# A hybrid attention block: block 2's search and four query projections moved, and attention's values as the stationary operand with probabilities in two parts

## The chip, the cores and the metric

One core of one Trainium2 chip runs the whole kernel in one launch. The metric is the device time in microseconds. The engines are TensorE (PE; PEld is its weight load), VectorE (DVE), ScalarE (ACT), GpSimd (POOL) and SyncE (SP), which issues the transfers. Each works through its own queue in order.

## The reference, cut to what matters

One layer of a decoder block on 1024 positions of 1024 channels, in float32. Half of the mixer's channels go through a gate over chunks of 128 positions, the other half through attention with 8 query heads of 64 and 2 key heads. An indexer scores the keys of each query, and the 256 highest are attended. A feed-forward stage of 4096 follows.

```python
score = jnp.einsum('bth,bths->bts', wb * (IDX_HEADS ** -0.5), jax.nn.relu(dots))
score = jnp.where(causal[None], score, -jnp.inf)
_, idx = lax.top_k(score, topk)                     # topk = 256
...
logits = jnp.einsum('btkgd,btjkd->btkgj', qg, kg) * (HEAD_DIM ** -0.5)
logits = jnp.where(sel_ok[:, :, None, None, :], logits, -jnp.inf)
p = jax.nn.softmax(logits, axis=-1).astype(v.dtype)
o = jnp.einsum('btkgj,btjkd->btkgd', p, vg)
...
merged = jnp.concatenate([rms_norm(y_a, g_out_sgu), rms_norm(y_b, g_out_attn)], axis=-1)
o = jnp.einsum('bse,ed->bsd', merged, w_out)
```

## The kernel before, in words

Queries stand in eight blocks of 128; block b sees b+1 blocks of keys. The stages in order of time: modulation, first norm and key projections (to about 100 us); the indexer's scores, the gates and the searches for the 256 best keys (to about 310); attention, with the first half of the output projection in its later part (to about 545); the second half, the second norm, and from about 640 us the feed-forward stage.

No list gives the order of the instructions. A scheduler sets it for each engine from the data's dependences and from priorities (`tc.cur_priority`, a smaller number is earlier), and each engine then takes its queue in that order. Tiles live in rings of buffers: `tr` (3 PSUM buffers for transposes), `pT` (2), `yb` (3), `raw` (2).

**The searches.** Blocks 0 and 1 take all their keys. For blocks 2 to 7 `select(b)` finds the threshold bit by bit, in 15 rounds. In a round the scores at or over the trial value are counted, the count is compared, and the trial value is changed. For blocks 6, 4 and 3 (`ON_ACT`) ACT counts (L615) and DVE does the two small steps (L616, L617); for 7, 5 and 2 DVE does all three (L603, L605, L607). The table `PRI` gives each block's search its priority. A few steps after the rounds (L637 to L646) prepare the lowest bits. `search_rest` (L648) then asks whether any row needs a longer search: L650 makes `more`, a matmul (L652) makes the flag, L653 copies it to `rest`, and a branch reads it (L657, L658). The longer search behind the branch is seldom needed and is not run here. The branch stands in a critical section, at which DVE waits for the other engines. The query projections `q_proj` of the last four blocks (24 matmuls each, L301 to L304) are made to follow the flag on PE. `mask(b)` (L671 to L686) turns a threshold into the bias `BI` by five passes over the block's scores; block 7's comes behind the branch, those of 6, 5, 4, 3 and 2 among the attention of blocks 7 and 1 (`MASKS`).

**The attention.** It runs over 32 units: blocks in the order `OB` = 0, 7, 1, 6, 5, 4, 3, 2, and for each two key heads (`grp`) and two pairs of query heads. A unit's logits (L730) are two fp32r matmuls for each 512 keys, added to the bias and reduced to the extreme on DVE (L731), then exponentiated on ACT (L734). The values follow for two key blocks at a time: four transposes of probabilities on PE (L769), one copy to SBUF on ACT (L750), and for each key block and head a matmul with the transposed probabilities as weights and 64 columns of float32 values moving (L755; it is shown as two instructions). After a block's two pairs L780 divides by the sum, `finish` normalises and transposes (L709 to L713), and from unit 19 on `oproj0` projects (L807 to L809). `stack_for` prepares the queries of a later unit (L322, L391, L392).

**Splitting in two.** The kernel has matmuls on float32 operands (L755) and on fp32r operands. For the latter a float32 operand is split into an upper half, rounded to fp32r (an ACT copy), and the rest, `lo` (a subtraction on DVE or POOL: L222, L392, L713, L882).

## Time and profile before

| what | value |
|---|---|
| time, median of 3 runs | 1246.16 us (1245.63 to 1246.74) |
| time of the profiled execution | 1248.28 us |
| its span, first to last instruction | 1246.4 us |
| mean granted TensorE clock | 0.967 of full speed |
| DVE instructions shown | 1798 |
| POOL instructions shown | 304 |

The profiled execution is 2.1 us over the median of the runs, and 1.9 us of it lie outside the span. A row of a timeline gives start and length in microseconds, engine, line and operation, output and input, and in brackets how long the engine stood idle before it and what released it. The length of a matmul's row is modelled and overlaps its successor's; the distance from one start to the next tells its rate. PEclk is the clock granted to TensorE as a share of full speed.

### The profile page before, as it was taken

What the parts mean: (1) busy time and instruction counts of PE and PEld (TensorE: products, weight loads), DVE (VectorE), ACT (ScalarE), POOL (GpSimd) and SP (SyncE); (2) the same over time, 40 slices, a digit from 0 to 9 for tenths busy, and PEclk for the clock granted to TensorE, in tenths of its full rate; (3) what the DMA queues carried; (4) which work ended last, traced back from release to release, by engine and by line L of the source; (5) the groups of instructions that cost most, each with busy time, mean ns of one, the idle gap of its engine ahead of it and who ended that gap; (6) DMA issues with size and microseconds to landing.
All of it is one profiled execution on the core that took longest, in us unless ns stands there. A gap on an engine that the chain in (4) does not pass through costs nothing.

```text
span 1246.4 us, 16883 instructions
## 1 busy us (share of the span) xinstructions
PE 1164.5 (93%) x5785; PEld 985.0 (79%) x5785; DVE 873.8 (70%) x1798; ACT 671.2 (54%) x1410; POOL 209.4 (17%) x304
## 2 busy tenths in 40 slices
PE   4899989995898999899899999999999999999997
PEld 4887768884697999887687788888887888888886
DVE  7844998968478666627898775655558756876568
ACT  4554679773266755537735455555544454445452
POOL 3585605451100000012610000000000000000001
PEclk9899989996898999999999999999999999999999
DMA  9431102110000144446315753544458455533335
GB/s 343 150 93 35 52 1 64 52 64 9 1 10 29 57 161 161 172 149 215 115 60 195 269 178 127 169 143 145 161 217 331 125 188 179 197 91 99 102 98 205
DMA packets 80239, 162.41 MB, mean 130 GB/s; under 512 B 7724, under 2 KB 32920, under 8 KB 80152
## 3 DMA queue, kind: packets, MB, share of 16 engines
q1 hardware_dynamic: 80136, 161.33, 38.3%
q8 instruction: 45, 0.74, 0.3%
q14 instruction: 42, 0.34, 0.1%
q10 hardware_dynamic: 16, 0.00, 0.0%
HBM read 119.36 MB, written 41.94 MB: 129 GB/s over the span
## 4 chain that ended last, share of the span: by engine, by line
PE 51%; DVE 12%; issue 4%; DMA 3%; ACT 2%; POOL 1%; SPq 0%; DVEq 0%; POOLq 0%; ACTq 0%
PE tr L1174 8%; PE lg L1174 8%; PE mm L1174 5%; PE mm L755 4%; PE lg L991 2%; PE lg L993 2%; PE lg L992 2%; PE tr L769 2%; PE lg L730 2%; PE tr L991 2%; PE tr L993 2%; PE tr L992 2%; DVE w L882 2%; PE mm L991 1%; PE mm L993 1%
## 5 line engine op out<-in xcount | busy, mean ns | idle before, releaser
L881 ACT ACTIVATE w<-rx 128x512 fp32r<-128x512 f32 x112 | 70.7, 632 | 148.1 <-PE lg L1174 64.5
L1174 PE MATMUL tr<-w,w 128*128 128x512 f32 x504 | 134.3, 392 | 2.9 <-DVE w L882 2.9
L1174 PE MATMUL lg<-w,w 128*128 128x512 f32 x504 | 133.7, 390 | 0.0
L882 DVE TENSOR_TENSOR w<-rx,w 128x512 fp32r<-128x512 f32 x112 | 77.2, 689 | 57.8 <-ACT w L881 57.1
L301 PE MATMUL mm<-w,hT 128*128 128x512 f32 (+1 forms) x288 | 112.8, 393 | 4.7 <-ACT hT L293 3.5
L1174 PEld LDWEIGHTS tr<-w,w 128*128 128x128 f32 x504 | 95.4, 189 | 23.2 <-DVE w L882 3.4
L303 PE MATMUL mm<-w,hT 128*128 128x512 f32 (+1 forms) x288 | 111.2, 387 | 0.0
L304 PE MATMUL mm<-w,hT 128*128 128x512 f32 (+1 forms) x288 | 110.2, 384 | 1.0 <-POOL hT L294 1.0
L1174 PEld LDWEIGHTS lg<-w,w 128*128 128x128 f32 x504 | 94.9, 188 | 19.7
L1210 POOL TENSOR_TENSOR rsf<-rsf,mhalf 128x1 f32<-128x1 f32 x8 | 6.0, 752 | 605.6 <-DVE rsf L1209 605.6
L1174 PE MATMUL mm<-w,w 128*128 128x512 f32 x336 | 93.9, 389 | 0.0
L755 PEld LDWEIGHTS mm<-VV,pT 128*128 128x128 f32 x576 | 76.1, 199 | 3.8 <-ACT pT L750 1.6
L755 PE MATMUL mm<-VV,pT 128*128 128x64 f32 x576 | 76.4, 277 | 0.9 <-ACT pT L750 0.9
L1174 PEld LDWEIGHTS mm<-w,w 128*128 128x128 f32 x336 | 63.1, 188 | 13.2
L882 DVE TENSOR_TENSOR w<-b,w 128x512 fp32r<-128x512 f32 x96 | 65.7, 685 | 4.0 <-ACT w L881 4.0
L301 PEld LDWEIGHTS mm<-w,hT 128*128 128x128 f32 x288 | 55.8, 194 | 14.9 <-ACT hT L293 3.7
L730 PE MATMUL lg<-KS,qs 128*128 128x512 f32 (+5 forms) x192 | 55.3, 399 | 10.6 <-DVE mxs L731 6.0
L882 DVE TENSOR_TENSOR w<-s,w 128x512 fp32r<-128x512 f32 x56 | 38.2, 688 | 37.3 <-ACT w L881 37.3
L304 PEld LDWEIGHTS mm<-w,hT 128*128 128x128 f32 x288 | 55.0, 191 | 10.5 <-POOL hT L294 1.3
L734 ACT ACTIVATE L<-L,mxs 128x128 f32<-128x128 f32 (+7 forms) x64 | 49.2, 771 | 25.8 <-DVE mxs L731 25.6
L881 ACT ACTIVATE w<-b 128x512 fp32r<-128x512 f32 x96 | 59.4, 618 | 6.7 <-DMA b<-in_w_ff_dram 6.5
L303 PEld LDWEIGHTS mm<-w,hT 128*128 128x128 f32 x288 | 55.5, 193 | 8.5
(356 smaller groups left out, 2975.5 us busy)
## 6 DMA issues: line engine op xcount, KB each, us to landing
rx<-x_scratch SPq DMA_DIRECT2D x56, 512.0 KB, 3.5
x_scratch<-d SPq DMA_DIRECT2D x108, 256.0 KB, 3.0
ada<-in_w_ada_dram SPq DMA_DIRECT2D x48, 512.0 KB, 5.6
raw<-in_w_ff_dram SPq DMA_DIRECT2D x32, 512.0 KB, 4.1
b<-in_w_ff_dram SPq DMA_DIRECT2D x32, 512.0 KB, 4.6
x<-in_x_dram SPq DMA_DIRECT2D x16, 512.0 KB, 5.6
raw<-in_w_in_dram SPq DMA_DIRECT2D x8, 512.0 KB, 3.6
raw<-in_w_in_dram SPq DMA_DIRECT2D x16, 256.0 KB, 2.8
```

The costliest lines, as they stand in the source:

```text
L301: mm = T.matmul(p[:, :n], lh, wt[k][:, 0, :n], start=k == 0, stop=False)
L303: T.matmul(p[:, :n], lh, wt[k][:, 1, :n], start=False, stop=False)
L304: T.matmul(p[:, :n], ll, wt[k][:, 0, :n], start=False, stop=k == KD - 1)
L730: T.matmul(pl, QS[b, grp][:, q, h4 * P:(h4 + 1) * P], KS[:, grp, c0:c0 + cw], start=q == 0, stop=q == 1)
L734: ex = A.activation(L, L, AF.Exp, scale=-1.0, bias=top, accum_out=sms[:, b, h:h + 1])
L755: mm = T.matmul(po[:, o:o + 64], e[:, (si * 2 + h2) * P:(si * 2 + h2 + 1) * P], VV[:, s0 + si, grp], start=first, stop=pair == 1 and s0 + ...
L881: A.activation(hi, src, AF.Copy)
L882: eng.tensor_tensor(lo, src, hi.bitcast(F32), op=OP.subtract)
L991: ms.append(T.matmul(p, a[:, 0, k], b[:, 0, k], start=start and k == 0, stop=False, skip_group_check=more))
L992: ms.append(T.matmul(p, a[:, 0, k], b[:, 1, k], start=False, stop=False, skip_group_check=more))
L993: ms.append(T.matmul(p, a[:, 1, k], b[:, 0, k], start=False, stop=stop and k == 3, skip_group_check=more))
L1174: ms.append(T.matmul(p, x[:, qa, t * P:(t + 1) * P], y[:, qb], start=start and n == 0, stop=stop and n == 2, skip_group_check=more))
```

## The change

1. **The search.** `PRI` gives block 2 the priority 445000 (it was 460000) and lists it before block 3. In `search_rest` the four query projections are written behind the critical section, no longer ahead of it.
2. **The values.** `VV` holds each value's upper and lower half beside each other, 128 columns, in fp32r; the lower half is one more DVE subtraction in each of eight key projections. The transposed probabilities are split too: `hi` by ACT, `lo` by DVE from PSUM, or, where `on_pool` says so, by POOL from a further ACT copy in the `raw` ring. A matmul now has the 128x128 `VV` as weights and 256 columns of probabilities (two heads) moving, once for `hi` and once for `lo` (L768). What comes out has the heads' outputs transposed, upper and lower half apart. So `values_T` copies it (ACT, into the `yb` ring), transposes it in four (L787), adds the halves in a reduction (L806) and multiplies (L807). It is called one unit later, and `finish` too.
3. **Room.** Some tiles of the gates go to a pool of their own, `gp`, which is closed before the searches; the `pT` buffers, twice as large, take its place (`pe`). Temporaries in `rotary` get one buffer each, and `mxs` is halved.

```diff
-    PRI = ((7, 400000), (6, 405000), (5, 415000), (4, 445000), (3, 455000), (2, 460000))
+    PRI = ((7, 400000), (6, 405000), (5, 415000), (4, 445000), (2, 445000), (3, 455000))
...
         V.tensor_copy(rest, p[:1, :1])
-        for b in OB[4:]:
-            q_proj(b, flag)
         with tc.tile_critical():
...
+        for b in OB[4:]:
+            q_proj(b, flag)
...
-        A.activation(VV[:, j], vv, AF.Copy)
+        A.activation(VV[:, j, :, 0:64], vv, AF.Copy)
+        V.tensor_tensor(VV[:, j, :, 64:128], vv, VV[:, j, :, 0:64].bitcast(F32), op=OP.subtract)
...
-            e = p2.tile([P, 512], F32, tag="pT", name=nm("pT"), bufs=2)
-            A.activation(e[:, :wd], pt[:, :wd], AF.Copy)
+            e = pe[0].tile([P, 2, 512], F32R, tag="pT", name=nm("pT"), bufs=2)
+            hi, lo = e[:, 0, :wd], e[:, 1, :wd]
+            if on_pool(u, s0):
+                r = rp.tile([P, 2, 512], F32, tag="raw", name=nm("pr"))[:, 0, :wd]
+                A.activation(r, pt[:, :wd], AF.Copy)
+                A.activation(hi, pt[:, :wd], AF.Copy)
+                G.tensor_tensor(lo, r, hi.bitcast(F32), op=OP.subtract)
+            else:
+                A.activation(hi, pt[:, :wd], AF.Copy)
+                V.tensor_tensor(lo, pt[:, :wd], hi.bitcast(F32), op=OP.subtract)
             for si in range(cnt_s):
-                for h2 in range(2):
-                    mm = T.matmul(po[:, o:o + 64], e[:, (si * 2 + h2) * P:(si * 2 + h2 + 1) * P], VV[:, s0 + si, grp],
+                for q in range(2):
+                    mm = T.matmul(po, VV[:, s0 + si, grp], e[:, q, si * 256:si * 256 + 256], start=first,
...
+    def on_pool(u, s0):
+        b = units[u][0]
+        if b < 2:
+            return False
+        return (s0 // 2) % 2 == 0 if b > 5 else s0 == 0 if b == 5 else u % 4 < 2
...
+    def values_T(b, grp):
+        oT = p2.tile([P, 512], F32, tag="yb", name=nm("oT"), bufs=3)
+        A.activation(oT, PO[b, grp], AF.Copy)
+        p = p_tr()
+        for i in range(4):
+            T.transpose(p[:, i * P:(i + 1) * P], oT[:, i * P:(i + 1) * P], ident)
...
     def normed(dst, src, b, h, n):
         V.reciprocal(sms[:, b, h:h + n], sms[:, b, h:h + n])
-        V.tensor_tensor(dst, src, sms[:, b, h:h + n, None].to_broadcast([P, n, 64]), op=OP.mult)
+        V.tensor_reduce(dst, src, op=OP.add, axis=mybir.AxisListType.X)
+        V.tensor_tensor(dst, dst, sms[:, b, h:h + n, None].to_broadcast([P, n, 64]), op=OP.mult)
...
+        if u and u % 2 == 0:
+            values_T(*units[u - 1][:2])
         values(u)
...
-        if u % 4 == 0 and u:
+        if u % 4 == 1 and u > 1:
             finish(OB[u // 4 - 1])
```

The scheduler then puts the instructions in another order. Lines of the changed kernel are numbered a few higher: L603 becomes L608, L616 L621, L731 L737.

On DVE, block 2's search before: its rounds (`self2`) stand behind the whole of block 3's and among the first steps of block 0's attention (`qs`, `L`).

```order
L603 TENSOR_SCALAR spare_903,self2_2640<-BI_87,self2_2640 128x384
L392 TENSOR_TENSOR qs_459_3012<-tr_461_3015,qs_459_3012 128x512
L605 TENSOR_SCALAR self2_2640<-self2_2640,kds_2636 128x1
L607 SCALAR_TENSOR_TENSOR self2_2640<-self2_2640 128x1
L731 ISA L_462_3022,mxs_3010<-lg_463_3023,BI_87 128x128
L731 ISA mxs_3010 128x1
L603 TENSOR_SCALAR spare_903,self2_2640<-BI_87,self2_2640 128x384
```

On DVE, the changed kernel: rounds of block 2 (`self2`) and of block 3 (`self3`) in turn.

```order
L608 TENSOR_SCALAR spare_913,self2_2654<-BI_87,self2_2654 128x384
L610 TENSOR_SCALAR self2_2654<-self2_2654,kds_2650 128x1
L621 TENSOR_SCALAR self3_2656<-self3_2656 128x1
L612 SCALAR_TENSOR_TENSOR self2_2654<-self2_2654 128x1
L622 SCALAR_TENSOR_TENSOR self3_2656<-self3_2656 128x1
L608 TENSOR_SCALAR spare_913,self2_2654<-BI_87,self2_2654 128x384
L610 TENSOR_SCALAR self2_2654<-self2_2654,kds_2650 128x1
```

All of block 2's rounds have moved ahead of block 0's attention, and they stand between block 3's.

On DVE, the end of the searches before: the flag's input `more` and the copy to `rest` follow the last search.

```order
L650 TENSOR_SCALAR more_2637<-kds_2636 128x6
L644 MAX self2_2640<-BI_87 128x8
L653 CAST rest_2638<-tr_496_3131 1x1
L646 ISA pick_2639,self2_2640<-pick_2639,self2_2640 128x8
L646 ISA self2_2640 128x1
L656 NO_OP
L1290 UNCONDITIONAL_BRANCH
L657 TENSOR_LOAD rest_2638
L658 COMPARE_AND_BRANCH
```

On DVE, the changed kernel, the same place: the steps just ahead of the copy to `rest` belong to block 0's attention; `more` (L655) stands 31 instructions earlier, ahead of its first `qs`.

```order
L737 ISA L_487_3115,mxs_3024<-lg_488_3116,BI_87 128x128
L737 ISA mxs_3024 128x1
L764 TENSOR_TENSOR pT_494_3136<-tr_493_3133,pT_494_3136 128x256
L807 TENSOR_TENSOR yb_491_3128<-yb_491_3128,sms_3025 128x256
L805 RECIPROCAL sms_3025<-sms_3025 128x4
L822 TENSOR_SCALAR ya_495_3141<-ya_495_3141,rsa_3021 128x512
L658 CAST rest_2652<-tr_498_3156 1x1
L659 NO_OP
L1322 UNCONDITIONAL_BRANCH
L660 TENSOR_LOAD rest_2652
L661 COMPARE_AND_BRANCH
```

The copy to `rest` and the branch have moved behind block 0's attention, whose steps no longer have a search between them.

On PE, the flag and the projections before, ahead of the branch of DVE:

```order
L709 MATMUL tr_495_3123<-ident_70,ya_493_3116 128x128 x4
L652 MATMUL tr_496_3131<-ones_75,more_2637 1x1
L301 MATMUL mm_497_3134<-w_428_2448,hT_12_143 128x512
L303 MATMUL mm_497_3134<-w_428_2448,hT_12_143 128x512
L304 MATMUL mm_497_3134<-w_428_2448,hT_12_143 128x512
L301 MATMUL mm_497_3134<-w_429_2451,hT_12_143 128x512
```

And in the changed kernel:

```order
L768 MATMUL mm_492_3132<-pT_494_3136,VV_83 128x256
L714 MATMUL tr_497_3148<-ident_70,ya_495_3141 128x128
L657 MATMUL tr_498_3156<-ones_75,more_2651 1x1
L301 MATMUL mm_499_3750<-w_428_2458,hT_12_143 128x512
L303 MATMUL mm_499_3750<-w_428_2458,hT_12_143 128x512
L304 MATMUL mm_499_3750<-w_428_2458,hT_12_143 128x512
L301 MATMUL mm_499_3750<-w_429_2461,hT_12_143 128x512
```

Nothing moved here: the projections (L301 to L304) follow the flag (L652, now L657) directly, though they are written behind the critical section.

On DVE, among the masks before: block 6's mask (`self6`) beside block 7's attention.

```order
L682 SCALAR_TENSOR_TENSOR SC_877<-eq_540_3975 128x896
L731 ISA L_546_4005,mxs_3010<-lg_548_4010,BI_87,mxs_3010 128x512
L731 ISA mxs_3010 128x1
L684 TENSOR_TENSOR self6_2648<-self6_2648,SC_877 128x1
L713 TENSOR_TENSOR mT_494_3122<-tr_542_3988,mT_494_3122 128x4x128
L685 SCALAR_TENSOR_TENSOR eq_540_3975<-SC_877,self6_2648,eq_540_3975 128x896
L686 SCALAR_TENSOR_TENSOR BI_87<-BI_87,eq_540_3975 128x896
L731 ISA L_561_4072,mxs_3010<-lg_562_4073,BI_87 128x512
```

And in the changed kernel:

```order
L687 SCALAR_TENSOR_TENSOR SC_884<-eq_546_4017 128x896
L814 TENSOR_SCALAR yb_491_3128<-yb_491_3128,rsb_3023 128x512
L689 TENSOR_TENSOR self6_2662<-self6_2662,SC_884 128x1
L690 SCALAR_TENSOR_TENSOR eq_546_4017<-SC_884,self6_2662,eq_546_4017 128x896
L764 TENSOR_TENSOR pT_545_4007<-tr_544_4002,pT_545_4007 128x512
L691 SCALAR_TENSOR_TENSOR BI_87<-BI_87,eq_546_4017 128x896
L764 TENSOR_TENSOR pT_557_4064<-tr_556_4059,pT_557_4064 128x512
L737 ISA L_568_4119,sms_3025<-lg_569_4120,BI_87 128x512
L737 ISA sms_3025 128x1
```

Subtractions (L764, the lower halves of probabilities) now stand between the mask's last passes and ahead of the logits' reductions.

## Rows read from the trace of the kernel before

**Rows 1.** The page: busy time, share and instructions of each engine

```profile
PE 1164.5 (93%) x5785; PEld 985.0 (79%) x5785; DVE 873.8 (70%) x1798; ACT 671.2 (54%) x1410; POOL 209.4 (17%) x304
```

**Rows 2.** Four stretches: length; PE, PEld, DVE, ACT, POOL; clock; DMA; GB/s

```profile
346.40:398.84 52.44, 48.48 (x365) 45.25 (x363) 47.91 (x135) 34.30 (x73) 4.62 (x9) 0.93 0.02 6
398.84:426.60 27.76, 25.46 (x214) 24.70 (x213) 19.70 (x54) 21.93 (x44) 2.03 (x3) 1.00 0.31 96
426.60:524.30 97.70, 96.70 (x666) 88.71 (x665) 61.08 (x138) 53.83 (x125) 4.83 (x8) 0.98 0.42 153
524.30:545.10 20.80, 18.50 (x104) 16.61 (x105) 10.07 (x19) 10.74 (x23) 2.96 (x3) 0.84 0.37 118
```

**Rows 3.** Timeline of DVE, 268 to 322 us: start, length, ..., [idle before]

```profile
268.77 0.21 DVE L616 TENSOR_SCALAR self<-self 128x1 f32<-128x1 f32 x1 [0.95 <-ACT spare L615]
...
270.12 0.21 DVE L616 TENSOR_SCALAR self<-self 128x1 f32<-128x1 f32 x1 [0.94 <-ACT spare L615]
...
287.80 0.69 DVE L392 TENSOR_TENSOR qs<-tr,qs 128x512 fp32r<-128x512 f32 x1
288.40 0.20 DVE L605 TENSOR_SCALAR self<-self,kds 128x1 f32<-128x1 f32 x1
...
303.96 0.61 DVE L603 TENSOR_SCALAR_CACHE_REDUCE spare<-BI,self 128x384 int8<-128x384 int16 x1
...
305.06 0.61 DVE L603 TENSOR_SCALAR_CACHE_REDUCE spare<-BI,self 128x384 int8<-128x384 int16 x1
...
310.36 0.13 DVE L653 CAST rest<-tr 1x1 int32<-1x1 f32 x1
...
321.01 0.15 DVE L671 CAST seli<-self 128x1 int32<-128x1 f32 x1 [10.36 <-DVEq L656]
```

**Rows 4.** Timeline of PE, 288 to 330 us

```profile
288.54 0.90 PE L730 MATMUL lg<-KS,qs 128*128 128x128 f32 x3 [3.66 <-DVE qs L392]
...
299.63 1.00 PE L709 MATMUL tr<-ident,ya 128*128 128x128 f32 x4
310.12 0.19 PE L652 MATMUL tr<-ones,more 128*1 128x1 f32 x2 [9.48 <-DVE more L650]
...
316.47 0.39 PE L303 MATMUL mm<-w,hT 128*128 128x512 f32 x1
...
329.43 1.22 PE L730 MATMUL lg<-KS,qs 128*128 128x512 f32 x2 [5.24 <-DVE mxs L731]
```

**Rows 5.** DVE queue's waits, 310 to 322 us: ns min/median/max, first, last

```profile
L1290 DVEq EVENT_SEMAPHORE  x6: 50/50/5610, 310.9 to 317.0; - x6
```

**Rows 6.** Timeline of PE, 371 to 374 us

```profile
371.70 0.60 PE L769 MATMUL tr<-ident,L 128*128 128x128 f32 x4
372.14 1.00 PE L755 MATMUL mm<-VV,pT 128*128 128x64 f32 x8
372.95 0.96 PE L730 MATMUL lg<-KS,qs 128*128 128x256 f32 x6
373.74 1.00 PE L755 MATMUL mm<-VV,pT 128*128 128x64 f32 x8
```

**Rows 7.** DVE by line, 345 to 400 us: busy us, mean ns

```profile
L392 DVE TENSOR_TENSOR qs<-tr,qs 128x512 fp32r<-128x512 f32 x4 | 2.8, 688 | 2.5 <-ACT qs L391 2.5
...
L780 DVE TENSOR_TENSOR yb<-mm,sms 128x256 f32<-128x256 f32 x4 | 1.7, 413 | 0.0
```

**Rows 8.** Groups of POOL by line and shape, whole span

```profile
L222 POOL TENSOR_TENSOR w<-raw,w 128x512 fp32r<-128x512 f32 x32 | 43.1, 1368 | 9.0 <-ACT w L221 7.6 <-PE mm L304 1.3
```

**Rows 9.** Timeline of POOL from 205.91 us

```profile
205.91 5.04 POOL L222 TENSOR_TENSOR w<-raw,w 128x512 fp32r<-128x512 f32 x4 [2.67 <-ACT w L221]
```

**Rows 10.** Timeline of DVE, 208 to 214 us

```profile
208.48 1.25 DVE L617 SCALAR_TENSOR_TENSOR self<-self 128x1 f32<-128x1 f32 x1
209.65 2.73 DVE L454 SCALAR_TENSOR_TENSOR SC<-relu,WI,SC 128x384 f32<-128x384 f32 x2
...
213.13 0.61 DVE L454 SCALAR_TENSOR_TENSOR SC<-relu,WI,SC 128x384 f32<-128x384 f32 x1
```

## What the change will do: the prediction

> **What bounds the kernel now.** The page's first part is read first: TensorE is busy 93% of the span and VectorE 70% [rows 1]. Those are averages, so the attention, where both halves of the change lie, is cut into stretches [rows 2]. Three different limits appear. From 346.4 to 398.84 us, where the last five masks are made beside the attention of blocks 7 and 1, DVE is busy 47.91 of 52.44 us and PE 48.48 at a clock of 0.93: both are nearly full, and DVE has 4.5 us to spare. From 398.84 to 426.6 PE is busy 25.46 of 27.76 and DVE 19.70. From 426.6 to 524.3 PE is busy 96.70 of 97.70 with DVE at 61.08: only PE's work counts there. The last 20.8 us are a tail in which each engine waits for another.
>
> Ahead of them stand the searches, for which DVE's and PE's timelines are read side by side [rows 3, 4]. A round of block 3's search, whose counting runs on ACT, takes 1.35 us (268.77 to 270.12), and in it DVE waits 0.95 us. Block 2's search follows on DVE, mixed from 287.80 with the first attention block; a round alone takes 1.10 us (303.96 to 305.06). PE waits 9.48 us for the end of these searches (310.12), and after the flag DVE stands still for 10.36 us until the first mask starts at 321.01. PE next waits 5.24 us for that mask (329.43).
>
> **The search (first half of the change).** Block 2's rounds go into the gaps of block 3's: by the order of DVE, one round of each in turn. A round's DVE work for block 2 is about 1.0 us (1.10 less the time between instructions) against a gap of 0.95 us, so the pair takes 1.4 to 1.5 us a round and both searches end about 291 (block 3's alone ended at 283). Block 0's attention then runs without search steps between. Before, it took from 287.80 to about 299.6, some 11.8 us (its last transposes on PE start at 299.63 [rows 4]) with six search rounds mixed in, and much of it was waiting between engines, as PE's 3.66 us for one `qs` shows [rows 4]. Alone, with its own new steps, I take 10.5 us. The flag's copy to `rest`, which now stands behind that chain on DVE, comes at 301.5 and not at 310.36 [rows 3]: a gain of 8.9 us, of which I take **8.5**. The bounds: 12 if block 0's chain shrinks to 7 us, 4 if the chain, alone, takes 15 us.
>
> The place of the four projections is priced at nothing. The wait behind the flag holds one semaphore wait of 5.61 us that begins at 311.3 [rows 5] and so ends at 316.9. That is when the twentieth projection matmul after the flag ends (it starts at 316.47 and is shown with 0.39 us) [rows 4]: the block's end waits for projections that the scheduler put ahead of it. In the order of the changed kernel the projections still stand directly behind the flag on PE, ahead of the same branch. So the 10.36 us stay. Were that wait really to go, 5.6 us more would be won; I bound that at 0 to 5.6 and take 0, because the rows of the order are the same.
>
> **TensorE's part of the attention.** Eight old value matmuls (128x64) take 0.81 us (372.14 to 372.95) and six 128x256 fp32r matmuls 0.79 (372.95 to 373.74) [rows 6]: 0.101 and 0.132 us each. For one key block and one pair of heads four of the first give way to two of the second: 0.404 less 0.263 is 0.141, and there are 144 such pieces: 20.3 us. Added are 64 transposes at 0.11 (four in 0.44, 371.70 to 372.14 [rows 6]): 7.0. PE wins 13.3 us in all, but only what falls where PE is the limit counts.
>
> **VectorE's part.** By the order of the changed kernel 13 subtractions of 128x512 and one of 128x256 (L764) and four reductions with a product each (L806, L807) fall between the stretch's start and the end of the last mask, one more such pair moves in from before it, and four products (L780) go. A subtraction with a PSUM input takes 0.688 us [rows 7], and its successor starts 0.60 after it (287.80 to 288.40 [rows 3]). So: 13 x 0.60 + 0.34, plus five times 0.69 for the reduction (no row has one: between L780's 0.413 and L392's 0.688, and nearest the latter, for it reads 512 elements from PSUM) and 0.38 for a product, less 4 x 0.413 [rows 7]: 7.8 + 0.3 + 5.4 - 1.7 = 11.8 us. DVE then has 59.7 us of work in a stretch of 52.44. PE gains some 5 us there, so part of DVE's 4.5 idle us goes: bound below 59.7 (+7.3), above 64.2 (+11.8). I take **+10**.
>
> From 398.84 to 426.6 DVE's additions of about 5 us fit beside PE; with some 22 of the 144 pieces and 8 transposes PE wins 3.1 - 0.9: **-2**. From 426.6 to 524.3 some 64 pieces and 36 transposes are 9.0 - 4.0 = 5.0 us of PE. DVE (61.08 now) goes to some 78 us, and ACT (53.83 now) has one copy more for each chunk that POOL splits and for each `oT`. Neither becomes the limit, but the lower half now comes through DVE's or POOL's queue, the new `oT` shares the three `yb` buffers, and a transposed chunk's PSUM buffer is held for two readers. That costs 1 to 4 us of new gaps; **-3** remains. In the tail one more transpose, copy and reduction stand in the chain: **+1** (-1 to +3). In the prelude eight subtractions of 128x128 (at most 8 x 0.413 us [rows 7]) run beside key projections: **+0.5** (0 to 3.3).
>
> **What POOL takes from DVE.** POOL gets 34 subtractions; its like takes 1.368 us [rows 8]. While four such ran from 205.91 [rows 9], two DVE operations L454 with all inputs in SBUF took 2.73 us, and one of the same shape later took 0.61 [rows 10]: each was more than doubled. In the masks' stretch ten of the subtractions meet L685 and L686, whose inputs are in SBUF too. If they meet by chance, 13.7 us of POOL in some 62 us hit about a fifth of 10 us of such DVE work: +2 us, already in the 10 above as a choice past the middle of its bounds. The Trainium skill, "SBUF — State Buffer", section "Who interferes with whom", speaks against the change: a DVE instruction with two SBUF inputs and a GpSimd instruction that reads SBUF exclude each other for the whole of the first one. By that rule each of ten meetings costs up to a full subtraction, some 14 us at worst in place of 2; it fits the 2.73 us, and is a rival below.
>
> **Sum.** -8.5 + 0.5 + 10 - 2 - 3 + 1 = -2 us. The profiled execution took 1248.28 us (span 1246.4), 2.1 above the median of the runs, 1246.16. Off the median the sum gives **1244.0**. About 2.5 us (0.2%) is what a measurement here can tell from no change, so the forecast lies just inside it.
>
> **Rivals.**
> *The masks' stretch pays more (slower).* Place: DVE, 346 to 399 us. Its queue is served in order, so a lower half behind a 2 us scan holds PE's value matmuls, and POOL's subtractions hold L685 and L686. For it: DVE's 47.91 of 52.44, and the 2.73 us. Against it: PE has 5 us to catch up. Price: the upper bound of 11.8 and half a subtraction for each of ten meetings, 6.8, make some 18 in place of 10, and block 0's chain, which has the same new steps, takes 13 us, so that 6 are won in place of 8.5: -6 + 0.5 + 18 - 2 - 3 + 1 = +8.5, 1254.5. It decides once the stretch costs over 13 us. Chance 0.22.
> *The earlier flag brings little.* Block 0's chain was paced by its own waits; if it takes 15 us alone, only 4 are won: 1248.5. Chance 0.17.
> *PE's saving comes through.* The late masks are needed only when their blocks come up (block 2 is last), so DVE may fall behind them without PE waiting; then the stretch costs 3 and not 10, and the PE-bound one wins 5 and not 3: 1235. For it: PE at 96.70 of 97.70 for half of the attention. Against it: the masks stand in the same queue as the logits that PE waits for. Chance 0.21.
> *The forecast's case*, 1240 to 1248: 0.40.
>
> **Chances.** Of the forecast's case I count 0.23 as faster by over 2.5 us, 0.12 within and 0.05 slower; with the third rival 0.44 are faster; the second splits in two, within and slower; the first is slower. Together 0.44 faster, 0.22 within, 0.34 slower. The range 1234 to 1256 takes in the rivals' times and leaves out the worst of the exclusion (14 us) and the free projections' 5.6 us on top of a gain. The likeliest case's own range is 1240 to 1248.
>
> **What would show it.** Right: block 2's and block 3's search steps alternate and end near 291; `rest` is copied near 301 and the first mask starts near 312; the 5.6 us semaphore wait stays; the last mask ends about 1 us later than before, as the 8.5 gained are spent on DVE at over 95% busy; the PE-bound stretch is 2 to 4 us shorter. Wrong: the last mask over 5 us later with L685 and L686 stretched (first rival); `rest` after 305 (second); DVE under 90% busy while PE stays full (third); or no long semaphore wait behind the flag, which would mean that the projections' place did count.

## The result, and the profile after

The changed kernel takes **1289.5 us** (median of 4 runs, 1286.78 to 1293.5), the kernel before 1245.89 on the same chip: a ratio of 1.036, 95% interval 1.0323 to 1.0397. It is slower by some 44 us, where 1244.0 was forecast and 1256 was the upper end of the range. The profiled execution took 1292.05 us, its span is 1290.3.

The page of the changed kernel: busy time of the engines, and the groups that answer to L755, L730 and POOL's new one.

```profile
PE 1169.3 (91%) x5561; PEld 969.1 (75%) x5561; DVE 925.1 (72%) x1868; ACT 697.7 (54%) x1460; POOL 258.3 (20%) x338
...
L768 PE MATMUL mm<-pT,VV 128*128 128x256 f32 x288 | 62.7, 322 | 22.6 <-DVE pT L764 11.7
L735 PE MATMUL lg<-KS,qs 128*128 128x512 f32 (+5 forms) x192 | 57.7, 403 | 21.6 <-DVE sms L737 11.3
...
L761 POOL TENSOR_TENSOR pT<-pr,pT 128x512 fp32r<-128x512 f32 (+1 forms) x34 | 47.4, 1402 | 112.8 <-ACT pT L760 106.5
```

Beside [rows 1] no engine has much more to do: DVE 51 us, POOL 49, ACT 27, and all three stay under 73%. What is new is 22.6 and 21.6 us in which PE stands idle ahead of the value and logit matmuls. The page of the kernel before had 0.9 and 10.6 there:

```profile
L755 PE MATMUL mm<-VV,pT 128*128 128x64 f32 x576 | 76.4, 277 | 0.9 <-ACT pT L750 0.9
L730 PE MATMUL lg<-KS,qs 128*128 128x512 f32 (+5 forms) x192 | 55.3, 399 | 10.6 <-DVE mxs L731 6.0
```

Where PE stands idle is seen with marks on DVE's timeline: the copy to `rest`, the first mask, the last mask, block 6's second product, block 2's last.

```profile
309.04 0.15 DVE L658 CAST rest<-tr 1x1 int32<-1x1 f32 x1 [0.60 <-PE tr L657]
317.90 0.15 DVE L676 CAST seli<-self 128x1 int32<-128x1 f32 x1 [8.71 <-DVEq L659]
...
412.01 0.54 DVE L691 SCALAR_TENSOR_TENSOR BI<-BI,eq 128x384 bf16<-128x384 bf16 x1
...
448.15 0.42 DVE L807 TENSOR_TENSOR yb<-yb,sms 128x256 f32<-128x256 f32 x1
...
578.90 0.42 DVE L807 TENSOR_TENSOR yb<-yb,sms 128x256 f32<-128x256 f32 x1
```

The same marks of each run divide its span into five stages (us):

| kernel | to first mask | masks' stretch | to block 6's end | to block 2's end | rest | span |
|---|---|---|---|---|---|---|
| before | 321.0 | 77.8 | 22.6 | 117.4 | 707.6 | 1246.4 |
| **changed** | 317.9 | 94.6 | 35.6 | 130.8 | 711.4 | 1290.3 |
| e1 search only | 308.6 | 77.2 | 23.7 | 117.6 | 709.5 | 1236.6 |
| e4 lower halves all by DVE | 317.8 | 90.0 | 26.0 | 118.0 | 710.1 | 1261.9 |
| e10 as e4, idle copies | 315.9 | 92.7 | 30.0 | 125.1 | 716.2 | 1279.9 |
| e11 POOL's copies kept, DVE subtracts, own ring | 317.5 | 91.8 | 25.1 | 130.5 | 710.1 | 1275.0 |
| e8 POOL's copies kept, DVE subtracts | 316.3 | 95.2 | 31.5 | 128.2 | 713.0 | 1284.2 |
| e3 own ring, POOL subtracts | 316.1 | 96.0 | 32.0 | 131.8 | 710.8 | 1286.7 |
| e7 no lower half | 316.5 | 79.3 | 22.0 | 106.6 | 712.6 | 1237.0 |

The changed kernel wins 3.1 us before the first mask and loses 16.8, 13.0, 13.4 and 3.8 behind it. In the kernels with the changed values a block's product comes one unit later, so the mark of block 6 is not quite the same place of the work as before; the third and fourth stage taken together are safer: 140.0 us before, 166.4 changed, 144.0 in e4.

**Block 6.** Queues show best here, since everything stops for 9 us. PE's timeline of the changed kernel, 428 to 438 us:

```profile
428.15 0.60 PE L795 MATMUL tr<-ident,L 128*128 128x128 f32 x4
437.33 1.01 PE L735 MATMUL lg<-KS,qs 128*128 128x384 f32 x2 [8.57 <-DVE sms L737]
```

DVE's, of the same place:

```profile
426.94 0.69 DVE L718 TENSOR_TENSOR mT<-tr,mT 128x512 fp32r<-128x512 f32 x1 [0.15 <-ACT mT L717]
429.36 1.43 DVE L225 SCALAR_TENSOR_TENSOR wo<-raw,cols,wo 128x512 fp32r<-128x512 f32 x2 [1.73 <-ACT wo L224]
432.02 1.41 DVE L225 SCALAR_TENSOR_TENSOR wo<-raw,cols,wo 128x512 fp32r<-128x512 f32 x2 [1.23 <-ACT wo L224]
435.38 1.42 DVE L225 SCALAR_TENSOR_TENSOR wo<-raw,cols,wo 128x512 fp32r<-128x512 f32 x2 [1.95 <-ACT wo L224]
436.71 0.55 DVE L737 CUSTOM_DVE_ANT_0 L<-lg,BI 128x384 f32<-128x384 f32 x1
```

ACT's:

```profile
428.60 1.33 ACT L224 ACTIVATE wo<-raw,cols 128x512 fp32r<-128x512 f32 x2 [1.70 <-DMA raw<-in_w_out_dram]
```

And what SP's queue waited for from 380 to 460 us (us in total, times, the longest):

```profile
SPq L819 <- DVE yb L814: 67.3, 3, 28.5
SPq L207 <- POOL pT L761: 8.6, 2, 6.3
```

Read backwards: PE's logits wait for a buffer that DVE has to empty (L737), DVE's L737 stands in its queue behind the splitting of the output weights (L225), that behind ACT's (L224), that behind the weights' transfer, and SP issues that (L207) only after the load of `ya` ahead of it in its queue (L819, which waits for a `yb` buffer that DVE's late L814 holds) and after POOL has read `pr` out of the two `raw` buffers (L761). Before, two of the four transfers of these weights had been issued at 260.46 and 265.15, ahead of the attention, and the others followed at 400.80 (260.98, 266.44 and 387.72 in e1), beside work that was there anyway. With the second `raw` user and the late `yb` all four come from 424.71 on.

**What it does to PE.** Windows of the changed kernel, masks' stretch from 364 on and the three behind it (length; PE, PEld, DVE, ACT, POOL; clock; DMA):

```profile
364.25:422.54 58.29, 42.08 (x250) 33.99 (x249) 51.52 (x129) 35.58 (x78) 15.13 (x14) 0.94 0.03 10
422.54:448.15 25.61, 15.26 (x89) 13.31 (x89) 16.15 (x39) 16.73 (x33) 5.65 (x5) 0.80 0.26 83
448.15:496.98 48.83, 44.27 (x268) 37.25 (x265) 36.65 (x84) 33.84 (x75) 18.49 (x15) 0.97 0.31 108
530.17:562.93 32.76, 28.14 (x147) 22.78 (x145) 23.40 (x41) 16.88 (x41) 5.97 (x5) 0.89 0.55 185
```

The first of them runs 10 us past the last mask. Up to that mask DVE is busy 46.1 of 48.3 us, so there DVE is nearly full. Behind it no engine is, where PE was at 96.70 of 97.70 before [rows 2]; and in the second and the last window, where PE stands idle for 10.4 of 25.6 and for 4.6 of 32.8 us, the granted clock is lower as well (0.80, 0.89).

### The profile page after: what moved, and what is told of

Its sections match the earlier page's. It is cut to its first block, busy times and chain, and to the rows that moved or that the text cites. A ratio compares the mean times of both kernels' runs of the same rounds, so it can differ in the third digit from the quotient of the medians.

```text
span 1290.3 us, 16614 instructions
## 1 busy us (share of the span) xinstructions
PE 1169.3 (91%) x5561; PEld 969.1 (75%) x5561; DVE 925.1 (72%) x1868; ACT 697.7 (54%) x1460; POOL 258.3 (20%) x338
## 4 chain that ended last, share of the span: by engine, by line
PE 54%; DVE 11%; ACT 4%; DMA 3%; issue 2%; POOL 1%; SPq 0%; DVEq 0%; POOLq 0%; ACTq 0%
PE tr L1206 8%; PE lg L1206 8%; PE mm L1206 5%; PE lg L1023 3%; PE lg L1024 3%; PE lg L1025 3%; PE tr L1023 3%; PE tr L1024 3%; PE tr L1025 3%; PE mm L834 2%; PE mm L835 2%; PE mm L836 2%; PE mm L1023 2%; PE mm L1024 2%; PE mm L1025 2%
## 5 line engine op out<-in xcount | busy, mean ns | idle before, releaser
L301 PE MATMUL mm<-w,hT 128*128 128x512 f32 (+1 forms) x288 | 113.1, 394 | 9.7 <-ACT hT L293 7.3
L304 PE MATMUL mm<-w,hT 128*128 128x512 f32 (+1 forms) x288 | 110.7, 386 | 0.3 <-POOL hT L294 0.3
L768 PE MATMUL mm<-pT,VV 128*128 128x256 f32 x288 | 62.7, 322 | 22.6 <-DVE pT L764 11.7
L735 PE MATMUL lg<-KS,qs 128*128 128x512 f32 (+5 forms) x192 | 57.7, 403 | 21.6 <-DVE sms L737 11.3
L301 PEld LDWEIGHTS mm<-w,hT 128*128 128x128 f32 x288 | 55.8, 194 | 21.5 <-ACT hT L293 7.5
L768 PEld LDWEIGHTS mm<-pT,VV 128*128 128x128 f32 x288 | 45.7, 202 | 34.5 <-DVE pT L764 15.5
L761 POOL TENSOR_TENSOR pT<-pr,pT 128x512 fp32r<-128x512 f32 (+1 forms) x34 | 47.4, 1402 | 112.8 <-ACT pT L760 106.5
L304 PEld LDWEIGHTS mm<-w,hT 128*128 128x128 f32 x288 | 55.4, 193 | 9.8 <-POOL hT L294 0.6
```

The lines of the kernel that those rows point to most:

```text
L301: mm = T.matmul(p[:, :n], lh, wt[k][:, 0, :n], start=k == 0, stop=False)
L304: T.matmul(p[:, :n], ll, wt[k][:, 0, :n], start=False, stop=k == KD - 1)
L735: T.matmul(pl, QS[b, grp][:, q, h4 * P:(h4 + 1) * P], KS[:, grp, c0:c0 + cw], start=q == 0, stop=q == 1)
L768: mm = T.matmul(po, VV[:, s0 + si, grp], e[:, q, si * 256:si * 256 + 256], start=first, stop=pair == 1 and s0 + si == ns - 1 and q == 1)
```

## The experiments

**e1, the first half alone.**

```diff
-    PRI = ((7, 400000), (6, 405000), (5, 415000), (4, 445000), (3, 455000), (2, 460000))
+    PRI = ((7, 400000), (6, 405000), (5, 415000), (4, 445000), (2, 445000), (3, 455000))
...
-        for b in OB[4:]:
-            q_proj(b, flag)
         with tc.tile_critical():
...
+        for b in OB[4:]:
+            q_proj(b, flag)
```

> The kernel before with the search part alone: block 2's priority and the place of the four projections. In the changed kernel's trace the first mask starts at 317.90 us and not at 321.01. If the search part is what it looks like there, and all of the loss lies in the values, this gives 3 us less than before, 1243. If the searches beside each other cost something later, or the early flag is given back at the masks, it gives 1246 or more. If they caused part of the loss of 43 us, over 1250.

Measured: 1234.35 us beside 1243.28, ratio 0.9916 (0.9885 to 0.9947): **9 us faster by the medians, and the fastest kernel of the study that leaves nothing out.** DVE's timeline of e1:

```profile
288.78 0.16 DVE L650 TENSOR_SCALAR_CACHE_REDUCE more<-kds 128x6 f32<-128x6 f32 x1
...
299.74 0.15 DVE L653 CAST rest<-tr 1x1 int32<-1x1 f32 x1 [1.07 <-PE tr L652]
308.61 0.15 DVE L671 CAST seli<-self 128x1 int32<-128x1 f32 x1 [8.72 <-DVEq L654]
```

The searches end at 288.8, block 0's chain takes 11 us, and the flag is copied 10.6 us earlier [rows 3]. The wait at the branch stays, at 8.7 us in place of 10.36. On PE the projections follow the flag directly in either kernel, so the gain is put down to the priority; it was not run apart.

**e2, the second half alone.** `PRI` and the projections' place as before.

> The changed kernel with the search part undone: the values' part alone. If the two parts add up, 1289.5 plus the 3 us that the search part wins: about 1292. If the loss needs both (the attention of block 0 with its lower halves standing ahead of the flag), it falls clearly under 1285.

Measured: 1298.97, ratio 1.0447 (1.0401 to 1.0494). The halves roughly add up: the second half costs 55.2 us beside e1 (1289.5 less 1234.35) and 55.7 beside the kernel before (1298.97 less 1243.28). All of the loss lies in it.

**e3, a ring of its own for POOL's copies; e4, no POOL.**

```diff
-                r = rp.tile([P, 2, 512], F32, tag="raw", name=nm("pr"))[:, 0, :wd]
+                if u <= 12:
+                    r = up.tile([P, 512], F32, tag="uv", name=nm("pr"), bufs=3)[:, :wd]
+                else:
+                    r = wp.tile([P, 1024], F32, tag="w", name=nm("pr"))[:, :wd]
```

> The changed kernel, but POOL's copies of the probabilities no longer use the two raw buffers through which the weights of the output projection come: up to unit 12 they use the three buffers of the gates' and masks' scratch, later the ring of twelve. Theory of the shared ring: the loads of these weights start at 424.71 us behind the last of POOL's copies in it, ACT and DVE stand still for them and PE waits 8.57 us at 437.33; with another ring the loads start before 400 as in the kernel before, and 9 to 14 us come back: 1276 to 1281. Theory that the loss is the lower half's way through the queues: the stall is only moved, at most 4 us come back.

```diff
     def on_pool(u, s0):
         b = units[u][0]
-        if b < 2:
+        if b < 8:
             return False
```

> The changed kernel with every lower half made on DVE from PSUM: no POOL subtraction, no second ACT copy, no copy in the raw ring; 34 subtractions more on DVE (30 x 0.60 + 4 x 0.34 us, about 19 us of DVE, some 5 of it in the masks' stretch). If POOL's holding up of DVE and the shared ring are the main loss, it gives 1265 to 1275. If DVE itself is the bound of the attention, it gives 1295 or more. If both weigh alike, about the time of the changed kernel.

Measured: e3 1287.99, 1.0361 (1.0319 to 1.0402), as the changed kernel. In e3 the first two transfers of the output weights are back at 269.02 and 274.76, and PE's longest wait between 400 and 450 us is 2.8 in place of 8.57; but block 6's stage is only 3.6 us shorter, and nothing of it reaches the end. So the stall was the most visible loss and not, by itself, the cause. e4 1264.22, 1.0184 (1.0135 to 1.0233). The route that was to spare DVE work costs 25 us more than DVE doing all of it. What e4 still loses is seen in its windows (the first from 364 to 16 us past the last mask, then three pieces of the late part):

```profile
364.19:423.40 59.21, 44.85 (x257) 35.23 (x258) 58.20 (x150) 37.14 (x79) 4.46 (x6) 0.94 0.13 45
...
433.75:480.87 47.12, 45.06 (x277) 37.87 (x275) 40.06 (x99) 30.30 (x65) 4.19 (x5) 1.00 0.32 112
480.87:511.87 31.00, 29.91 (x185) 25.89 (x184) 26.08 (x55) 18.02 (x42) 3.06 (x3) 1.00 0.47 161
511.87:540.35 28.48, 24.79 (x150) 20.73 (x149) 24.16 (x47) 17.57 (x40) 1.59 (x1) 1.00 0.57 194
```

In the first DVE is full, 58.20 of 59.21. In the late part PE is busy 109.3 us (these three rows and 9.5 in the last 11.4). The late part of the kernel before:

```profile
421.39:464.19 42.80, 42.80 (x322) 40.52 (x320) 26.18 (x68) 25.26 (x56) 3.05 (x5) 1.00 0.33 112
464.19:494.58 30.39, 30.39 (x198) 27.57 (x197) 18.97 (x40) 15.83 (x38) 1.17 (x2) 0.94 0.44 165
494.58:522.20 27.62, 27.62 (x185) 24.98 (x184) 17.64 (x39) 14.84 (x38) 1.16 (x2) 1.00 0.48 182
522.20:538.78 16.58, 13.28 (x68) 11.61 (x67) 9.91 (x18) 10.81 (x22) 1.11 (x1) 0.79 0.38 120
```

PE is busy 114.1 us in it and idle 3.3; in e4 it is idle 8.8. So the saving of 4.8 stands as idle time beside it. (Part of the 4.8 is the clock's: it was granted at 0.96 before and at 1.00 in e4.)

**e8 and e11, what of the route is POOL.** POOL's subtraction is done by DVE from the same copy: in e8 with the shared `raw` ring, in e11 with e3's own ring.

```diff
-                G.tensor_tensor(lo, r, hi.bitcast(F32), op=OP.subtract)
+                V.tensor_tensor(lo, r, hi.bitcast(F32), op=OP.subtract)
```

> The changed kernel with POOL's 34 subtractions given to DVE, on the same copies: ACT still copies these probabilities twice, the first time into the raw ring, and only POOL itself is out. The kernel with all lower halves on DVE from PSUM took 1264, the changed one 1289.5. If POOL's slow subtraction and its holding up of DVE make that difference: 1264 to 1270. If the second ACT copy and the raw ring make it: 1282 to 1290. The ring's stall alone was seen as 8.57 us of PE: then about 1275.

> The kernel with POOL's 34 subtractions on DVE but the second copy left (1284.8), its copies now out of the raw ring (scratch of the masks up to unit 12, then the ring of twelve). If the raw ring holds up the output projection's weights and that is what those copies cost: 1268 to 1275. If the second copy itself is the cost: 1280 to 1285.

Measured: e8 1284.79, 1.0325 (1.0292 to 1.0358); e11 1277.5, 1.0271 (1.0232 to 1.0311), between its two theories. With e3 and the changed kernel that is a table of two by two: POOL 1289.5 and 1288.0, DVE 1284.8 and 1277.5 (shared ring, own ring). The ring alone is worth 7 us once DVE subtracts, and hardly anything beside POOL; POOL itself 5 to 10; and the second copy, which e11 still has and e4 has not, 13. (They come from several sets of runs, whose times of the kernel before lie between 1243.3 and 1245.9, so differences of 2 or 3 us are not to be read from this, and the 5 is near that limit: the intervals of the changed kernel and of e8 overlap.)

What POOL does to DVE stands in DVE's groups from 325 to 600 us. The changed kernel:

```profile
L483 DVE SCALAR_TENSOR_TENSOR adacc<-ada,cact,adacc 128x1024 f32<-128x1024 f32 x21 | 32.1, 1527 | 0.5 <-DMA ada<-in_w_ada_dram 0.2
...
L681 DVE TENSOR_TENSOR self<-seli,self 128x1 f32<-128x1 f32 x5 | 2.9, 583 | 0.0
...
L687 DVE TENSOR_TENSOR_SCAN SC<-eq 128x768 f32<-128x768 bf16 x1 | 2.8, 2819 | 0.0
...
L690 DVE SCALAR_TENSOR_TENSOR eq<-SC,self,eq 128x768 bf16<-128x768 f32 x1 | 1.9, 1921 | 0.0
```

and e8:

```profile
L483 DVE SCALAR_TENSOR_TENSOR adacc<-ada,cact,adacc 128x1024 f32<-128x1024 f32 x21 | 26.8, 1278 | 0.1
...
L687 DVE TENSOR_TENSOR_SCAN SC<-eq 128x768 f32<-128x768 bf16 x1 | 1.7, 1748 | 0.0
...
L690 DVE SCALAR_TENSOR_TENSOR eq<-SC,self,eq 128x768 bf16<-128x768 f32 x1 | 1.0, 1019 | 0.0
...
L681 DVE TENSOR_TENSOR self<-seli,self 128x1 f32<-128x1 f32 x5 | 0.8, 153 | 0.0
```

All four read two operands from SBUF. L690 takes 0.9 us longer and L687 1.1. L681, of one element a row, takes 583 ns on average in place of 153: two of its five took 1.25 and 1.24 us, the others 0.13 to 0.15. Each of these four, and one more of L690 (128x896, 2.06 us in place of 1.14), began less than 0.25 us after a subtraction of POOL's had begun. The five meetings cost DVE 5.1 us in the masks' stretch. The Trainium skill, "SBUF — State Buffer", section "Who interferes with whom", says that a DVE instruction with two SBUF inputs contends with a GpSimd instruction that reads SBUF, and calls what they share an exclusive lock; these rows agree. The dearest group is one that the prediction did not look at: L483, 5.3 us over 21 instructions. How much of either reaches the end of the kernel was not tried apart.

**e10, idle copies.** e4, with 34 further ACT copies of the same chunks that nothing reads.

```diff
+                if twice(u, s0):
+                    jk = p2.tile([P, 512], BF, tag="jb", name=nm("jk"), bufs=1)
+                    A.activation(jk[:, :wd], pt[:, :wd], AF.Copy)
                 A.activation(hi, pt[:, :wd], AF.Copy)
```

> The kernel with all lower halves on DVE from PSUM (1264), and in it 34 further ACT copies of the probabilities that nobody reads, where the changed kernel copies twice: about 20 us of ACT. If ACT's time, and the copies that wait behind in its queue, make the second copy dear: 1272 to 1285. If the copy costs only as a link of the chain (the lower half waits for both copies), nothing waits for this one: 1264 to 1267.

Measured: 1279.33, 1.0282 (1.0244 to 1.032): 15 us over e4 for copies of 19.5 us, in a kernel where ACT is busy 54%. The idle copy is written ahead of its chunk's upper half, and by the order of ACT's rows it is taken first in all 34 cases; ACT's timeline of e10 shows the first of them:

```profile
343.91 0.60 ACT L765 ACTIVATE jk<-tr 128x512 bf16<-128x512 f32 x1 [1.19 <-PE tr L804]
344.40 0.59 ACT L766 ACTIVATE pT<-tr 128x512 fp32r<-128x512 f32 x1
```

So nothing has to wait for the copy's result, and it needs neither POOL nor the `raw` ring to be dear: it is enough that it takes its turn on ACT ahead of the copy that PE's matmuls and `lo` wait for, 0.5 us where the two follow each other directly. That makes the way from probabilities to `lo` longer by one copy, as in e11. It also keeps the transposed chunk (`tr`, three PSUM buffers) longer; how the 15 us divide between the later upper half and `tr` was not tried apart.

**e7, no lower half of the probabilities.** Upper half alone: the copy, the subtraction and half of the value matmuls are left out, and with them that part of the product.

> The changed kernel without the lower half of the probabilities: no subtraction, no POOL copy, one matmul with the upper half for each key block in place of two (144 matmuls, some 19 us of PE, fewer). It leaves that part of the computation out. Values as weights, their own split, the transposes of the output and the reductions stay. Theory that the lower half's way through the queues is the loss: 1220 to 1235, under the kernel before. Theory that the new output path (copy, transposes, reduction, one unit later) costs as much: 1250 or more.

Measured: 1236.35, 0.9928 (0.9908 to 0.9949). Without the second part attention loses nothing on balance: the masks' stretch is 79.3 us, and the late part is 10.8 us shorter than before. But e7 leaves out PE's work too: PE is busy 98.8 us in the late part, 15.3 less than before, and idle 7.9 where it was idle 3.3. So it is not shown that the values as weights, the transposes of `oT` and the later `finish` cost nothing: some 4.5 us of new idle time stand there without the second part, whose cause was not tried apart. The larger loss in attention is the second part of the probabilities and what carries it.

**The prelude: e9, e12b, e13, e15.** In the changed kernel the searches end (`more`) at 296.0, in e1 at 288.8. e9 leaves out the lower half of the values (L378; the upper stands in its place); e12b gives the temporaries in `rotary` two buffers again; e13 does both; e15 does both with e4's `on_pool`.

```diff
-         A.activation(VV[:, j, :, 0:64], vv, AF.Copy)
-         V.tensor_tensor(VV[:, j, :, 64:128], vv, VV[:, j, :, 0:64].bitcast(F32), op=OP.subtract)
+         A.activation(VV[:, j].rearrange("p h (w e) -> p h w e", w=2), vv[:, :, None, :].to_broadcast([P, 2, 2, 64]), AF.Copy)
...
-            n_ = t0.tile([P, 64], F32, tag="rn", name=nm("n"), bufs=1)
+            n_ = t0.tile([P, 64], F32, name=nm("n"))
```

> The changed kernel without the eight subtractions that make the lower half of the values: ACT writes the upper half into both places, so the values' lower half is left out. In the changed trace the key projections end 5.5 us later than before, with PE idle for 4.6 us and then at half clock. If these subtractions cause that: 1283 to 1285. If it comes from the temporaries of the rotary tables with one buffer: no change, 1289.

> The changed kernel with the rotary tables' temporaries in two buffers each again (the positions' tile stays shared). In the changed trace the second half of these steps waits for the sine of the first, and the norm's steps behind it on DVE start 1.8 us later (46.97 in place of 45.18), which grows to 5.5 us by 90 us. If the single buffers cause that: 4 to 6 us less than the changed kernel, 1284 to 1287 beside 1290. If the shared positions' tile or the values' split does: no change.

> The changed kernel with both of its additions before 100 us taken away: the rotary temporaries have two buffers each again, and the lower half of the values (the DVE subtraction) is left out, the upper half standing in its place. If these two are the whole of the prelude's loss and add up, the first search pass starts near 127 us (133.3 in the changed kernel, 126.9 with the search's change alone) and the first qs of block 0 near 289 (296.9). Rival: the cause is a third thing (the pools moved), then the first qs stays above 293. What comes of it at the end: 1282 to 1286 if it is handed on, 1289 if the later stages use it up in waits, as when only one of the two was taken away.

> The same, and all lower halves of the probabilities by DVE, so that POOL's route is gone too (the lower half of the values is left out as before). With all by DVE alone it was 1264.2. If the prelude's 7 to 8 us are handed on by a DVE-bound chain: 1256 to 1258. If something in between uses them up: 1262 to 1264. What then remains over the version with the search's change alone (1234) would be the masks' stretch and block 0's chain, 15 to 22 us.

Measured: e9 1291.79, 1.039 (1.0349 to 1.0431); e12b 1287.02, 1.0348 (1.031 to 1.0385); e13 1291.09, 1.0384 (1.0362 to 1.0405); e15 1267.37, 1.0195 (1.0167 to 1.0222). None is measurably faster than its partner, the changed kernel or e4. Yet the place was right. PE's timeline of the changed kernel, 68 to 77 us:

```profile
68.81 0.31 PE L303 MATMUL mm<-w,hT 128*128 128x328 f32 x1
68.96 0.31 PE L304 MATMUL mm<-w,hT 128*128 128x328 f32 x1
71.79 0.55 PE L322 MATMUL tr<-ident,kv 128*128 128x128 f32 x3 [2.52 <-POOL kv L317]
74.42 0.90 PE L322 MATMUL tr<-ident,kv 128*128 128x128 f32 x3 [2.08 <-POOL kv L317]
75.45 0.61 PE L301 MATMUL mm<-w,hT 128*128 128x328 f32 x1
75.86 0.47 PE L303 MATMUL mm<-w,hT 128*128 128x328 f32 x1
76.13 0.47 PE L304 MATMUL mm<-w,hT 128*128 128x328 f32 x1
```

Two waits of 2.5 and 2.1 us, and behind them matmuls at 0.27 us each (75.86 to 76.13), where the two before the waits stand 0.15 apart. In e13 the waits are down to 0.4 and 1.7 us and the slow matmuls are gone: from 70 to 85 us PE is busy 14.17 of 15 at full clock (changed kernel: 11.00 at 0.77). DVE's first step on the indexer's scores shows what each addition costs up to there: 111.45 us in the changed kernel, 104.99 in e1, 105.67 without the values' lower half (e9), 108.45 with two `rotary` buffers (e12b), 104.88 with both (e13). Behind it the gain is lost again: `more` comes at 295.1 in e9, 293.6 in e12b and 295.9 in e13. DVE's waits from 100 to 290 us show where e13's went:

```profile
DVE SC L455 <- ACT relu L451: 15.4, 11, 3.3
```

and in e1:

```profile
DVE SC L454 <- ACT relu L450: 8.7, 6, 3.7
```

DVE waits longer for ACT in the indexer's scores (10.9 us in the changed kernel). Why the order that the scheduler made is worse there stays open; the tiles moved to `gp` are left as a candidate that wasn't tried.

## Why the prediction was wrong, by its steps

- **The search (-8.5): right by itself.** The rounds alternate, in e1 the searches end at 288.8 (291 was said) and the flag is copied at 299.74 (301 to 301.5); e1 gained 9. The price of nothing for the projections' place was near: the wait behind the flag went from 10.4 to 8.7 us, the semaphore wait in it from 5.61 to 3.99. In the changed kernel, though, `rest` is copied at 309.04, behind the 305 that was named as the sign of the second rival. Its reason, a block 0 chain of 15 us, holds in part: the chain takes 13.0 us there, 11.0 in e1.
- **The prelude (+0.5, at most 3.3): wrong, 7.** The eight subtractions were sized by their length and taken to lie beside other work. At the first step on the scores the changed kernel is 6.5 us behind e1, and leaving the subtractions out (e9) gives 5.8 of it back. The buffers halved in `rotary` were not priced at all; two again (e12b) give 3.0. `more` comes 7.2 us later than in e1; with the 2.1 of block 0's chain that leaves 1.3 of the search's gain when `rest` is copied (309.04, before 310.36). That neither addition, taken out, makes the kernel faster is the open part: the scores' stage uses up what was won.
- **The masks' stretch (+10): the mechanism was right, the size low.** DVE is the limit, as was said, and its new steps were counted nearly right: 15 subtractions (9.7 us) and five reductions (3.4, at the 0.69 foretold) came in, 13.1 us beside 11.8. The stretch before and in the changed kernel (there without the last 0.54 us; DVE is the third number after the length):

```profile
321.01:398.84 77.83, 68.63 (x447) 61.59 (x446) 62.42 (x165) 40.76 (x85) 8.70 (x19) 0.91 0.01 4
317.90:412.01 94.11, 70.85 (x380) 56.85 (x378) 79.72 (x186) 49.79 (x102) 22.60 (x29) 0.93 0.02 6
```

  What the +10 missed is that POOL's hold took 5.1 us in place of 2, and that DVE's idle time hardly shrank to pay for any of it (15.4 us before, 14.4 changed). Against e1, e4 loses 12.8 us and the changed kernel 17.4. The rival "pays more" had 18 here, for these reasons, and with it 1254.5 in all: the place was the rival's, and more was lost behind it.
- **398.8 to 426.6 (-2): wrong, +13.** That DVE's additions "fit beside PE" counted busy time. What moved was the transfer of the output weights, held by the `raw` ring and by the load ahead of it in SP's queue. A ring of its own takes the 8.57 us wait away, but shortens the stage by 3.6 only (e3), and by 10.5 when DVE also subtracts (e11). The prediction had looked the queues up for the projections, not for the copies in `raw`.
- **The PE-bound part (-3): wrong, +13.4, and with the stage before it the largest error.** PE's own work came out near the forecast in e4: 109.3 us in place of 114.1, 4.8 against 5.0 foretold. "Neither becomes the limit" was true by busy time (DVE 96 of 118 us in e4) and didn't decide. The new gaps were put at 1 to 4 us. With DVE alone PE's idle time grew by 5.5 and took the whole saving. In the changed kernel it grew by 10.3 (3.3 to 13.6), and PE's work was not shorter either: busy 117.2 us at a granted clock of 0.93 (0.96 before, 1.00 in e4). A slower clock beside the gaps stood in no step. Both stages behind the masks together show whose gaps they are: 144.0 us with DVE alone, 155.1 with idle copies on ACT (e10), 155.6 with the real ones in a ring of their own (e11), 163.8 with POOL subtracting from them (e3), 166.4 in the changed kernel. So the second copy on ACT is the largest single part, and POOL the next; e7 shows that some 4.5 us of gaps stay without the second part.
- **The tail (+1): 3.8**, outside its bounds of -1 to +3. But this stage runs to the end of the kernel, and reads 1.9 more than before in e1 too, where nothing in the tail was changed.
- **POOL's hold on DVE (+2, at worst 14):** POOL costs 5 to 10 us by e8 and e11. On DVE 5.1 us of it are seen in the masks' stretch and 5.3 in L483, which stood in no step. The prediction's rows gave 2.73 us for two L454 together; that each of them was doubled, as it said, they don't show.

The third rival, that PE's saving comes through, fell: PE no longer was full where it should have paid.

## What to carry to other kernels

An engine at 97% busy lives on the lead that the others have over it. Before work is added to the chain that feeds it, count for each chunk the queues that it passes and the buffers that it shares, and not only the busy shares: 19.5 us of idle copies, ahead of those that PE waits for, on an engine at 54% cost 15 us here. A ring that holds prefetched weights is a poor place for a working copy, since whatever holds it holds the transfer, and behind that the queues of three engines; but removing the stall that shows best (8.57 us here) can leave the time as it was. And work that is handed to POOL to spare DVE has to be weighed with every DVE instruction that reads two operands from SBUF in that time, those of other stages too.

## What was not expected of the hardware

DVE's timeline of the changed kernel at 405 us:

```profile
405.07 1.24 DVE L681 TENSOR_TENSOR self<-seli,self 128x1 f32<-128x1 f32 x1
```

and POOL's:

```profile
405.00 1.29 POOL L761 TENSOR_TENSOR pT<-pr,pT 128x512 fp32r<-128x512 f32 x1 [8.56 <-ACT pT L760]
```

They begin within 0.07 us and end together: a DVE instruction on one element a row took 1.24 us beside POOL's subtraction, where e8 shows 0.153. What a meeting costs did not go by the size of the DVE instruction: 1.1 us for one element a row, 0.9 to 1.1 for 768 or 896 of them. The kernel before had shown it: in [rows 10] L617, on one element a row, takes 1.25 us at 208.48 while POOL subtracts (its median is 0.16), and the prediction read only the L454 beside it. That e13 took more than half of PE's 4.6 us of waits before 76 us away, with full clock behind them, and left the end of the searches 220 us later where it was, was the other surprise.
